# Queries and keys: rounded and subtracted over 128 rows, halves moved by transfers

## The chip, the core and the metric

One core of one Trainium2 chip. PE multiplies matrices, DVE and ACT work on tiles of 128 rows (partitions), POOL and SP here mostly issue transfers (DMAs). All are driven by instruction streams of their own, in an order fixed when the kernel is built, and wait for each other by semaphores. The metric is the device time of one execution in microseconds, the median of three runs.

## The reference

One step of a decoder layer in fp32, for 1024 prompt tokens and 8 x 8 sample tokens together (T = 1088 columns).

```python
xn = rmsnorm(x, norm1_g)
q, k, v, glu_a, glu_b, gate_a, gate_b = split(xn @ w_in)       # 16 query heads, 4 key heads of 64
attn = swa(q, k, v, sinks)                                      # window 128, a learned sink a head
c = dwconv31(glu_a * sigmoid(glu_b))                            # causal depthwise convolution
merged = sigmoid(gate_a) * (attn @ w_o_attn) + sigmoid(gate_b) * (silu(layernorm(c)) @ w_pb)
h = x + merged @ w_out
y = h + (silu(gate) * val) @ w_down                             # gate, val = dwconv3(rmsnorm(h) @ w_up)
return rmsnorm(y)                                               # and the new caches
```

## The kernel before

Every fp32 product is made of three matmuls in the rounded format fp32r: an operand is split in a high half (the value rounded) and a low half (the value minus the high half), and PE adds wh x xh, wh x xl and wl x xh (lines 201 to 203). A split is a cast on ACT and a subtract on DVE (`split_ps`, lines 230 and 231; for weights lines 182 and 183).

The first phase streams the columns of `w_in` as 128-wide weights through PE, each over the tokens in three chunks (0 to 384, 384 to 768, 768 to 1088), eight steps a chunk. The order of the weights is a table of letters: b and a (the two factors of the conv input), g (gates), q, k, v. It starts `b a q0 g q0`, five weights side by side while the input is being normed, and goes on `b a q0 q0 k0 b a v v g g ...`; later stand `q1 q1 q1 g q1 k1`. The digit is the head pair p (0 or 1), and a q weight holds two query heads j of it, one in rows 0 to 63 and one in rows 64 to 127. After the projections of a pair come its scores (lines 359 and 360: kd and kl times q), softmax (330 to 339), transposes (369, split at 231 into `pth` and `ptl`) and the product with v (381 to 388), between the weights that follow.

Scores take q with its high and low halves stacked over the 128 rows: in the tile `q0` (g = 0) the high half of the head is in rows 0 to 63 (`r` in the code) and the low half in rows 64 to 127 (`x`), in `q1` (g = 1) the other way round. `kd` holds the high half of a key head in both halves of the rows, `kl` the low half in both. So values have to change rows. Before, the engines do this by reading PSUM in one half of the rows and writing in the other (lines 730 and 731 for q, 751 to 755 for k). In the opening the scaled PSUM goes through a tile `qt` (line 834), which then stands for the PSUM.

Beside it run the conv of each channel group (chains on DVE at line 483; its input `u`, two buffers, is cleared by POOL at lines 662 and 663 and gets its history by the SP load `u<-cbT` at 664; its result goes out by POOL at 506 and 507) and the folds of the out weights (line 616, POOL copies and adds in memory). Weights are loaded by SP (`wraw<-wall`, line 159).

A scheduler sets the order in each engine's stream, from priorities and its own estimates; an instruction of a later weight can stand ahead of one of an earlier one. A tile has as many buffers as its pool says, and an instruction that writes a buffer waits for the last reader of it, a transfer included. SP and POOL issue their transfers in stream order, so one that waits holds up all behind it.

Of the kernel before, what the change touches and what calls it, by code (L numbers as in the profile page):

```python
# [6 lines left out]
F32 = mybir.dt.float32  # L7
F32R = mybir.dt.float32r
AF = mybir.ActivationFunctionType
ALU = mybir.AluOpType  # L10
AX = mybir.AxisListType

P = 128
# [107 lines left out]
class Build:  # L121
# [517 lines left out]
    def pool(self, es, name, side="right", bufs=1):  # L639
        return es.enter_context(self.tc.tile_pool(name=name, bufs=bufs, side=side, reuse_waits="tile"))  # L640

    def phase_x(self):
        nc, tc, a, pool = self.nc, self.tc, self.a, self.pool
# [5 lines left out]
        gl = pool(right, "gl")  # L649
# [56 lines left out]
        def gate_evac(kind, i):  # L706
# [8 lines left out]
                nc.gpsimd.dma_start(dst[i, :, o:o + n], t[:, :n])  # L715
            return ev

        def q_evac(p, j):
            st = states[p]
            if j == 0:  # L720
                st["q"] = [self.t(qp, [P, 4, T], f"q{g}", F32R) for g in range(2)]
                st["qs"] = self.t(qp, [P, NB // 2, 3 * 8 * NT], "qs")
                nc.gpsimd.memset(st["qs"], 0.0)

            def ev(c, o, n, ps):
                m = min(n, SEQ - o)
                for g in range(2):
                    r, x = [slice(y * HD, (y + 1) * HD) for y in (g, 1 - g)]
                    q = st["q"][g][:, j, o:o + m]
                    nc.scalar.copy(q[r], ps[r, :m])  # L730
                    nc.vector.tensor_tensor(q[x], ps[r, :m], q[r].bitcast(F32), ALU.subtract)  # L731
                if m < n:
                    for g in range(2):
                        r = slice(g * HD, (g + 1) * HD)
                        row = st["qs"].rearrange("p a (s x) -> p a s x", s=3)[r, :, 0:3:2]
                        nc.scalar.copy(row[:, :, :, (4 * g + j) * NT:(4 * g + j + 1) * NT],
                                       ps[r, m:n].rearrange("p (a s t) -> p a s t", a=NB // 2, s=2))
            return ev

        def do_k(p):  # L740
            st = states[p]
            st["ks"] = self.t(kv, [P, NS], "ks")
            st["kd"] = [self.t(kv, [P, SEQ], f"kd{g}", F32R) for g in range(2)]
            st["kl"] = [self.t(kv, [P, SEQ], f"kl{g}", F32R) for g in range(2)]

            def ev(c, o, n, ps):
                m = min(n, SEQ - o)
                for g in range(2):
                    r, x = [slice(y * HD, (y + 1) * HD) for y in (g, 1 - g)]
                    kd = st["kd"][g][:, o:o + m]  # L750
                    nc.scalar.copy(kd[r], ps[r, :m])
                    kl = st["kl"][g][:, o:o + m]
                    nc.vector.tensor_tensor(kl[r], ps[r, :m], kd[r].bitcast(F32), ALU.subtract)
                    nc.scalar.copy(kd[x], ps[r, :m])  # L754
                    nc.scalar.copy(kl[x], kl[r].bitcast(F32))
                if m < n:
                    nc.scalar.copy(st["ks"], ps[:, m:n])
                    kf = self.t(gl, [P, 384], "gt", bufs=2)[:, :WIN]
                    nc.scalar.copy(kf, ps[:, m - WIN:m])
                    nc.gpsimd.dma_start(a["o_kp"][p], kf)  # L760
                    nc.gpsimd.dma_start(a["o_kn"][p], st["ks"])

            self.stream(("k", p), xs, ev)
# [38 lines left out]
        p0_es = ExitStack()  # L802
        p0 = pool(p0_es, "p0", "left")
        put_q = [q_evac(0, j) for j in range(2)]
        spare = [q[:, 3, :DM] for q in states[0]["q"]]
        self.slot = lambda i: (None, spare) if i == 4 else (p0, "xy"[i - 2]) if 2 <= i < FIRST else (self.wp, i % 2)
# [32 lines left out]
        for c in range(3):  # L839
# [3 lines left out]
            r, steps = self.norm1_stats(p0, c, xr[c])  # L843
# [36 lines left out]
        for n, (kind, i) in enumerate(self.order[:self.n_in]):  # L880
# [16 lines left out]
            if kind == "b":  # L897
                u = do_b(i)
            elif kind == "a":
                do_a(i, u)  # L900
            elif kind in ("ga", "gb"):
                self.stream((kind, i), xs, gate_evac(kind, i))
            elif kind == "q":
                if i == (1, 0):
                    self.drain()
                self.stream((kind, i), xs, q_evac(*i))
            elif kind == "k":
                do_k(i)
                if i == 1:
                    plan_units(1)  # L910
            elif kind == "v":
                if i == 0:
                    do_v()
                    plan_units(0)
# [892 lines left out]
```

## Time and profile before

| | us |
|---|---|
| runs, median (lowest, highest) | 1663.01 (1662.69, 1663.13) |
| profiled execution | 1661.67 |
| its span | 1659.9 |
| PE busy | 1641.4 |
| DVE busy | 1338.7 |
| ACT busy | 892.3 |
| POOL busy | 318.4 |

A row of a group in the profile reads: line, engine, operation, output <- inputs, number; then durations in ns (smallest, median, largest) or the sum and the mean. A row of a timeline: start, duration, engine, line, operation, and in brackets the idle time ahead of it with what ended it. A row of a stretch gives the busy us of PE, weight loads, DVE, ACT and POOL with their numbers of instructions, then PE's granted clock, the DMA engines' share and GB/s. The granted clock is 1.00 in the stretches shown.

### The profile page before, as it was taken

The page shows a single profiled execution, that of the slowest core. Times are in us where ns is not written, and L with a number is a line of the kernel's source. Part 1 is how long each engine was busy: PE and PEld are TensorE (multiplying, and loading weights), DVE is VectorE, ACT ScalarE, POOL GpSimd, SP SyncE. Part 2 cuts the span into 40 slices and gives each one's busy share as a digit, 9 for nine tenths or more (in the row PEclk, how much of TensorE's full clock was granted, in tenths as well). Part 3 has the DMA queues.
Part 4 walks back from the last instruction along what each step waited for, and adds up shares of the span by engine and source line. Part 5 has one row for each costly group of instructions (what it writes and reads, how often), then busy time and mean ns, then how long its engine had stood idle before and what let it go on. Part 6 is the DMA issues. An engine that isn't in the chain of part 4 may idle for free.

```text
span 1659.9 us, 30349 instructions
## 1 busy us (share of the span) xinstructions
PE 1641.4 (99%) x11616; PEld 1623.9 (98%) x11616; DVE 1338.7 (81%) x2432; ACT 892.3 (54%) x1819; POOL 318.4 (19%) x589
## 2 busy tenths in 40 slices
PE   9999999999999999999999999999999999999998
PEld 9999899999999999999999999999999999999998
DVE  8999988999769995875676897877777778968546
ACT  7524377753388754993353564444444446834322
POOL 0400222151211211110000123333433221000050
PEclk9999999999999999999999999999999999999999
DMA  6122135163421255545346527676777544856473
GB/s 213 46 48 71 60 94 136 48 200 82 124 67 49 66 192 189 176 137 187 120 126 204 134 71 212 182 182 176 182 176 176 144 112 142 288 158 220 137 147 119
DMA packets 121746, 232.12 MB, mean 140 GB/s; under 512 B 25457, under 2 KB 68097, under 8 KB 121169
## 3 DMA queue, kind: packets, MB, share of 16 engines
q1 hardware_dynamic: 88496, 140.01, 27.4%
q0 software_dynamic: 32384, 89.51, 21.3%
q8 instruction: 91, 1.49, 0.4%
q10 hardware_dynamic: 720, 0.66, 0.1%
q14 instruction: 55, 0.44, 0.1%
HBM read 169.74 MB, written 89.62 MB: 156 GB/s over the span
## 4 chain that ended last, share of the span: by engine, by line
PE 83%; DVE 11%; ACT 3%; DMA 1%; issue 1%; SPq 0%; DVEq 0%; ACTq 0%
PE mm L201 20%; PE mm L202 20%; PE mm L203 20%; PE aux L201 6%; PE aux L203 6%; PE aux L202 6%; DVE c L483 3%; DVE bt L483 1%; PE aux L369 1%; DMA xr<-xT 1%; DVE q L731 1%; PE aux L359 1%; DVE wlo L183 1%; PE aux L381 1%; DVE xr L307 1%
## 5 line engine op out<-in xcount | busy, mean ns | idle before, releaser
L201 PE MATMUL mm<-xh,whi 128*128 128x384 f32 (+1 forms) x920 | 306.7, 333 | 2.9 <-ACT kd L754 1.6
L203 PE MATMUL mm<-xh,wlo 128*128 128x384 f32 (+1 forms) x920 | 300.6, 327 | 0.0
L202 PE MATMUL mm<-xl,whi 128*128 128x384 f32 (+1 forms) x920 | 300.5, 327 | 0.0
L201 PEld LDWEIGHTS mm<-xh,whi 128*128 128x128 f32 x920 | 173.0, 188 | 5.1 <-ACT kd L754 1.9
L202 PEld LDWEIGHTS mm<-xl,whi 128*128 128x128 f32 x920 | 173.2, 188 | 0.8
L203 PEld LDWEIGHTS mm<-xh,wlo 128*128 128x128 f32 x920 | 172.7, 188 | 0.1
L1225 DVE SCALAR_TENSOR_TENSOR acc<-st,fc,acc 128x1104 f32<-128x1104 f32 x88 | 119.5, 1362 | 8.7 <-ACT acc L1223 7.9
L182 ACT CAST whi<-wraw 128x1024 fp32r<-128x1024 f32 (+1 forms) x65 | 62.6, 969 | 55.8 <-PE mm L202 49.6
L483 DVE SCALAR_TENSOR_TENSOR bt<-u,consts,bt 128x513 f32<-128x513 f32 x120 | 89.7, 748 | 0.6
L483 DVE SCALAR_TENSOR_TENSOR c<-sm,hsum,c 128x512 f32<-128x512 f32 x120 | 89.5, 746 | 0.5
L183 DVE TENSOR_TENSOR wlo<-wraw,whi 128x1024 fp32r<-128x1024 f32 (+1 forms) x65 | 73.3, 1134 | 20.1 <-ACT whi L182 19.7
L483 DVE SCALAR_TENSOR_TENSOR c<-u,consts,c 128x512 f32<-128x512 f32 x112 | 83.5, 746 | 0.3
L230 ACT CAST wlo<-th 128x512 fp32r<-128x512 f32 x56 | 35.1, 626 | 65.1 <-PE aux L203 41.4
L1394 ACT COPY st<-mm 128x272 f32<-128x272 f32 (+2 forms) x133 | 44.4, 350 | 46.7 <-PE mm L203 46.7
L201 PE MATMUL mm<-th,whi 128*128 128x272 f32 x240 | 69.3, 289 | 0.0
L203 PE MATMUL mm<-th,whi 128*128 128x272 f32 x240 | 69.3, 289 | 0.0
L202 PE MATMUL mm<-tl,whi 128*128 128x272 f32 x240 | 69.1, 288 | 0.0
L335 ACT ACTIVATE p<-p,nm 128x257 f32<-128x257 f32 (+1 forms) x128 | 62.2, 490 | 12.0 <-DVE nm L330 11.2
L1373 DVE TENSOR_TENSOR st<-st,aux 128x272 f32<-128x272 f32 (+2 forms) x95 | 34.2, 379 | 38.0 <-PE aux L203 38.0
L203 PE MATMUL mm<-sh,wlo 128*128 128x384 f32 (+1 forms) x192 | 62.6, 326 | 0.0
L202 PE MATMUL mm<-sl,whi 128*128 128x384 f32 (+1 forms) x192 | 62.6, 326 | 0.0
L201 PE MATMUL mm<-sh,whi 128*128 128x384 f32 (+1 forms) x192 | 62.6, 326 | 0.0
(651 smaller groups left out, 5896.1 us busy)
## 6 DMA issues: line engine op xcount, KB each, us to landing
wraw<-wall SPq DMA_DIRECT2D x87, 512.0 KB, 3.9
d_x<-st POOLq DMA_DIRECT2D x27, 544.0 KB, 5.3
d_wd<-wall POOLq DMA_DIRECT2D x54, 256.0 KB, 6.2
th<-wall SPq DMA_DIRECT2D x18, 512.0 KB, 6.2
wraw<-wall SPq DMA_DIRECT2D x33, 256.0 KB, 4.3
x<-d_x SPq DMA_DIRECT2D x14, 544.0 KB, 4.6
d_x<-acc POOLq DMA_DIRECT2D x9, 816.0 KB, 7.3
d_wo<-wall POOLq DMA_DIRECT2D x24, 256.0 KB, 4.8
```

The lines of the kernel that those rows point to most:

```text
L182: self.nc.scalar.copy(h[:, z], r[:, z])
L183: self.nc.vector.tensor_tensor(l[:, z], r[:, z], h[:, z].bitcast(F32), ALU.subtract)
L201: mm(ps, wh, xh, start=first, stop=False, skip_group_check=more)
L202: mm(ps, wh, xl, start=False, stop=False, skip_group_check=more)
L203: mm(ps, wl, xh, start=False, stop=last, skip_group_check=more)
L230: self.nc.scalar.copy(h, src)
L307: nc.vector.scalar_tensor_tensor(x, x, self.c("g1", k), rstd[:, :CHUNKS[c][1]], ALU.mult, ALU.mult)
L335: nc.scalar.activation(pt[:, j, lo:width + 1], pt[:, j, lo:width + 1], AF.Exp, bias=nm[:, j:j + 1], scale=-1.0, accum_out=den[:, j:j + 1])
L483: mac = lambda o, x, w: nc.vector.scalar_tensor_tensor(o, x, w, o, ALU.mult, ALU.add)
L1225: self.last_tap = nc.vector.scalar_tensor_tensor(acc, st[:, k:k + AW], fw(f, k), acc, ALU.mult, ALU.add)
L1373: plus = lambda d, s: nc.vector.tensor_tensor(d, d, s, ALU.add)
L1394: op(d, r(ps))
```

## The change

A new function `both_parts` splits a chunk's PSUM (or `qt`) over all 128 rows into two tiles `qkh` and `qkl`, one buffer each: one cast and one subtract. Transfers issued by SP then carry 64-row halves of them to where they belong: four a chunk for q (high and low, for two g), eight a chunk for k (high and low, each to both halves of the rows, for two g). For a q chunk one cast on ACT and one subtract on DVE go, for a k chunk five casts or copies on ACT and one subtract on DVE. Over 24 q chunks and 6 k chunks these are 54 fewer on ACT and 30 fewer on DVE, and 144 transfers more. The copies of sample tokens (`qs`, `ks`) and the new caches stay on ACT.

The diff touches only this; the norm matmuls of the opening stand at the same places in both kernels.

```diff
+        def both_parts(ps, m):
+
+            h, l = [self.t(gl, [P, 384], f"qk{z}", F32R) for z in "hl"]
+            self.split_ps(h[:, :m], l[:, :m], ps[:, :m])
+            return h, l
+
         def q_evac(p, j):
...
                 m = min(n, SEQ - o)
+                parts = both_parts(ps, m)
                 for g in range(2):
                     r, x = [slice(y * HD, (y + 1) * HD) for y in (g, 1 - g)]
                     q = st["q"][g][:, j, o:o + m]
-                    nc.scalar.copy(q[r], ps[r, :m])
-                    nc.vector.tensor_tensor(q[x], ps[r, :m], q[r].bitcast(F32), ALU.subtract)
+                    for z, part in zip((r, x), parts):
+                        nc.sync.dma_start(q[z].bitcast(F32), part[r, :m].bitcast(F32))
...
                 m = min(n, SEQ - o)
+                parts = both_parts(ps, m)
                 for g in range(2):
                     r, x = [slice(y * HD, (y + 1) * HD) for y in (g, 1 - g)]
-                    kd = st["kd"][g][:, o:o + m]
-                    nc.scalar.copy(kd[r], ps[r, :m])
-                    kl = st["kl"][g][:, o:o + m]
-                    nc.vector.tensor_tensor(kl[r], ps[r, :m], kd[r].bitcast(F32), ALU.subtract)
-                    nc.scalar.copy(kd[x], ps[r, :m])
-                    nc.scalar.copy(kl[x], kl[r].bitcast(F32))
+                    for to, part in zip((st["kd"], st["kl"]), parts):
+                        for z in (r, x):
+                            nc.sync.dma_start(to[g][z, o:o + m].bitcast(F32), part[r, :m].bitcast(F32))
```

Line 664 and the lines up to 717 keep their numbers; below, the lines of the kernel after are 5 or 6 higher. The order on PE is the same in both kernels. On the other engines the scheduler has moved work; three places follow.

On DVE, at the first two chunks of the third query head of p=0 (mm is PSUM; c, bt, sm and u belong to the conv chain). Before:

```order
L483 SCALAR_TENSOR_TENSOR c_883<-sm_884,hsum_86,c_883 128x512
L483 SCALAR_TENSOR_TENSOR bt_885<-u_165,consts_77,bt_885 128x513
L731 TENSOR_TENSOR q_26_122<-mm_1203,q_26_122 64x384
L483 SCALAR_TENSOR_TENSOR c_883<-u_165,consts_77,c_883 128x512
L731 TENSOR_TENSOR q_27_123<-mm_1203,q_27_123 64x384
L483 SCALAR_TENSOR_TENSOR c_883<-sm_884,hsum_86,c_883 128x512
L483 SCALAR_TENSOR_TENSOR bt_885<-u_165,consts_77,bt_885 128x513
L483 SCALAR_TENSOR_TENSOR c_883<-u_165,consts_77,c_883 128x512
L731 TENSOR_TENSOR q_26_122<-mm_1232,q_26_122 64x384
L483 SCALAR_TENSOR_TENSOR c_883<-sm_884,hsum_86,c_883 128x512
L731 TENSOR_TENSOR q_27_123<-mm_1232,q_27_123 64x384
L483 SCALAR_TENSOR_TENSOR bt_885<-u_165,consts_77,bt_885 128x513
```

After:

```order
L483 SCALAR_TENSOR_TENSOR bt_909<-u_165,consts_77,bt_909 128x513
L483 SCALAR_TENSOR_TENSOR c_907<-u_165,consts_77,c_907 128x512
L231 TENSOR_TENSOR qkl_1253<-mm_1227,qkh_1252 128x384
L483 SCALAR_TENSOR_TENSOR c_907<-sm_908,hsum_86,c_907 128x512
L483 SCALAR_TENSOR_TENSOR bt_909<-u_165,consts_77,bt_909 128x513
L483 SCALAR_TENSOR_TENSOR c_907<-u_165,consts_77,c_907 128x512
L483 SCALAR_TENSOR_TENSOR c_907<-sm_908,hsum_86,c_907 128x512
L483 SCALAR_TENSOR_TENSOR bt_909<-u_165,consts_77,bt_909 128x513
L231 TENSOR_TENSOR qkl_1286<-mm_1260,qkh_1285 128x384
L483 SCALAR_TENSOR_TENSOR c_907<-u_165,consts_77,c_907 128x512
L483 SCALAR_TENSOR_TENSOR c_907<-sm_908,hsum_86,c_907 128x512
L483 SCALAR_TENSOR_TENSOR bt_909<-u_165,consts_77,bt_909 128x513
```

The two subtracts of a chunk with a conv row between them have become one, and conv rows stand where the second one was: between the subtracts of the two chunks there are five of them now, three before between the last of one and the first of the next. Ahead of the first `ptl` on DVE there stand 111 rows of line 483 before and 119 after.

On SP, at the last query head of p=1 and its keys. Before (the weights around the load of the last u of this stretch):

```order
L159 DMA wraw_4457<-wall 128x1024
L159 DMA wraw_4553<-wall 128x1024
L159 DMA wraw_4645<-wall 128x1024
L159 DMA wraw_4747<-wall 128x1024
L664 DMA u_5538<-cbT 128x8x30
L159 DMA wraw_4862<-wall 128x1024
L159 DMA wraw_5067<-wall 128x1024
```

After:

```order
L738 DMA q_548_4321<-qkl_4639 64x256
L738 DMA q_549_4322<-qkl_4639 64x256
L159 DMA wraw_4741<-wall 128x1024
L159 DMA wraw_4855<-wall 128x1024
L664 DMA u_5658<-cbT 128x8x30
L738 DMA q_548_4321<-qkh_4772 64x384
L738 DMA q_549_4322<-qkh_4772 64x384
L738 DMA q_548_4321<-qkl_4773 64x384
L738 DMA q_549_4322<-qkl_4773 64x384
L738 DMA q_548_4321<-qkh_4805 64x384
L738 DMA q_549_4322<-qkh_4805 64x384
L738 DMA q_548_4321<-qkl_4806 64x384
```

The four transfers of each chunk of that head (`qkh_4772` and `qkl_4773` are its first chunk's) and the eight of each chunk of k1 behind them stand after the load of `u`, where before only weights stood.

On POOL, at the conv store and the folds ahead of that load's memset (lines 662 and 663). Before:

```order
L616 DMA d_wo_65<-wall 128x512 x2
L507 DMA d_c_59<-u_4019 128x64
L616 DMA d_wo_65<-d_wo_65 16x4096
L616 DMA d_wo_65<-wall 128x512 x2
L506 DMA d_c_59<-u_4019 128x1024
L616 DMA d_wo_65<-wall 128x512
L662 MEMSET u_5538 128x30
L663 MEMSET u_5538 128x2
L616 DMA d_wo_65<-d_wo_65 16x4096
```

After:

```order
L507 DMA d_c_59<-u_4079 128x64
L616 DMA d_wo_65<-d_wo_65 16x4096
L506 DMA d_c_59<-u_4079 128x1024
L616 DMA d_wo_65<-wall 128x512
L715 DMA d_gb_61<-gt_4736 128x320
L616 DMA d_wo_65<-wall 128x512 x2
L616 DMA d_wo_65<-d_wo_65 16x4096
L662 MEMSET u_5658 128x30
L663 MEMSET u_5658 128x2
```

The stores of the conv result (507 and 506) and a fold's copy (`d_wo<-d_wo`) stand earlier against the moves from the weights (`d_wo<-wall`, a copy or an add), a gate's store stands behind them, and a second `d_wo<-d_wo` is now ahead of the memset.

## The prediction

> **What bounds the kernel.** I began with the first part of the page, busy time by engine.
>
> ```profile
> span 1659.9 us, 30349 instructions
> PE 1641.4 (99%) x11616; PEld 1623.9 (98%) x11616; DVE 1338.7 (81%) x2432; ACT 892.3 (54%) x1819; POOL 318.4 (19%) x589
> ```
>
> PE is busy for 1641.4 of 1659.9 us, and its 11616 matmuls stay as they are. The change can win only where PE waits, and can lose wherever PE is made to wait. The second view lists what PE waited for (total, number of times, longest).
>
> ```profile
> PE aux L359 <- DVE ptl L231: 3.5, 2, 3.0
> PE aux L299 <- DVE rows L314: 1.7, 2, 1.4
> PE mm L201 <- ACT kd L754: 1.6, 1, 1.6
> PE mm L201 <- ACT qs L736: 1.3, 1, 1.3
> ```
>
> The last two are waits for the lines that the change rewrites, so it is tempting to book 2.9 us. The third view, busy time by stretch (PE, weight loads, DVE, ACT, POOL), says why not.
>
> ```profile
> 100.00:120.00 20.00, 20.00 (x124) 20.00 (x123) 19.65 (x32) 3.69 (x7) 1.46 (x2) 1.00 0.22 34
> 120.00:140.00 20.00, 18.68 (x111) 18.11 (x110) 19.47 (x29) 9.01 (x20) 1.25 (x4) 1.00 0.28 87
> 140.00:160.00 20.00, 18.44 (x114) 18.12 (x113) 19.15 (x28) 11.50 (x24) 1.09 (x2) 1.00 0.25 76
> 180.00:200.00 20.00, 19.96 (x139) 19.23 (x138) 19.86 (x43) 10.39 (x32) 3.78 (x7) 1.00 0.24 70
> 200.00:220.00 20.00, 16.01 (x96) 14.39 (x95) 19.54 (x44) 15.15 (x41) 5.81 (x8) 1.00 0.18 64
> 260.00:300.00 40.00, 40.00 (x261) 38.96 (x260) 39.13 (x87) 31.16 (x80) 11.25 (x22) 1.00 0.42 110
> 400.00:440.00 40.00, 40.00 (x243) 40.00 (x242) 39.15 (x60) 11.79 (x26) 3.76 (x7) 1.00 0.25 75
> 440.00:460.00 20.00, 20.00 (x130) 20.00 (x129) 9.82 (x22) 12.60 (x26) 4.65 (x9) 1.00 0.69 159
> ```
>
> From 100 to 220 DVE has no idle time left (19.2 to 19.9 of each 20 us), PE has. So in this stretch DVE sets the pace, and the last place at which PE waits long for it is the one that counts: what PE loses earlier it would otherwise lose there. From 260 on PE is full in every stretch shown, so what is won before 260 stays won, unless a new wait appears. The timeline shows that last place.
>
> ```profile
> 202.91 0.33 PE L203 MATMUL mm<-xh,wlo 128*128 128x384 f32 x1
> 206.24 0.39 PE L359 MATMUL aux<-kd,q 128*128 128x256 f32 x1 [3.00 <-DVE ptl L231]
> ...
> 204.83 0.75 DVE L483 SCALAR_TENSOR_TENSOR c<-u,consts,c 128x512 f32<-128x512 f32 x1
> 205.50 0.69 DVE L231 TENSOR_TENSOR ptl<-aux,pth 128x512 fp32r<-128x512 f32 x1
> ```
>
> The attention of the first pair p=0 has begun; PE needs a bank that DVE's `ptl` still reads, and DVE reaches `ptl` only after a run of conv rows (L483), one each 0.665 us (204.83 to 205.50).
>
> **The DVE term, a gain.** The tiles q, kd and kl give the prices.
>
> ```profile
> L730 ACT CAST q<-mm x36: 365/473/478, 101.4 to 446.7; 64x384 fp32r<-64x384 f32 x24, 64x256 fp32r<-64x256 f32 x12
> L731 DVE TENSOR_TENSOR q<-mm,q x36: 417/552/560, 109.5 to 447.1; 64x384 fp32r<-64x384 f32 x24, 64x256 fp32r<-64x256 f32 x12
> L753 DVE TENSOR_TENSOR kl<-mm,kd x12: 416/549/561, 135.1 to 459.4; 64x384 fp32r<-64x384 f32 x8, 64x256 fp32r<-64x256 f32 x4
> L754 ACT CAST kd<-mm x12: 353/472/480, 135.7 to 460.9; 64x384 fp32r<-64x384 f32 x8, 64x256 fp32r<-64x256 f32 x4
> ```
>
> A 64-row subtract becomes half of a 128-row one with as many elements to a row; the 128-row conv rows next to it are timed by their row length too, so I price the new one like one old one (0.55 us at 384, 0.42 at 256), and each chunk saves one subtract. Up to that `ptl` there are 15 chunks: three each of the two opening heads, of heads 2 and 3, and of k. Ten are 384 wide and five 256: 10 x 0.55 + 5 x 0.42 = 7.6 us. But the scheduler fills the place: ahead of this `ptl` stand 111 conv rows before and 119 after. Eight more of them take 8 x 0.665 = 5.3 us. What is left is 2.3 us, and I take 2.5, since several of the removed rows also came with a short wait for their own cast. At most the 3.0 us of the wait above can be won here, with 0.5 us more at its other entry (3.5 in total); at least nothing, if DVE now waits for transfers to free its tile. ACT loses 54 short casts; it is the bound nowhere in these stretches (3.7 to 15.2 of 20), so I cost them at nothing.
>
> **The transfers.** They are new: 144 on SP's queue, 4 to a q chunk and 8 to a k chunk. No transfer from tile to tile is in this trace, so their price comes from neighbours.
>
> ```profile
> 0.74 0.87 SPq L257 DMA_DIRECT2D xr<-xT  x2
> 1.66 0.42 SPq L255 DMA_DIRECT2D wraw<-wall  x1
> ```
>
> ```profile
> d_ga<-gt POOLq DMA_DIRECT2D x4, 192.0 KB, 2.6
> ...
> o_kp<-gt POOLq DMA_DIRECT2D x1, 64.0 KB, 1.8
> ```
>
> Issuing takes SP 0.43 us each, 0.45 with the step to the next. Landing took 1.8 us for 64 KB and 2.6 for 192 KB (medians of two stretches); a half of 64 x 384 has 98 KB and lies nearer the first: 1.8 us, at most 2.6. One page bears on both numbers: the Trainium skill, "DMA: Bandwidth & Descriptors", section "Anatomy of one DMA — SWDGE (gpsimd) path", gives a fixed 2.0 us plus bytes over 436 GB/s, 2.2 us for 98 KB as an estimate, inside the two rows; by that the chain below would be 1.6 us longer. The same table gives some 50 ns for a dispatch, on POOL's path, where SP's rows show 0.43 a transfer; by it the twelve issues in the chain below would take 4.8 us less, and the whole would come to 1662.
>
> On an idle queue the transfers are hidden: a chunk is 24 matmuls, about 4 us of PE (243 in 40 us from 400 to 440), and a chunk's high halves need cast 0.47, two issues 0.9 and landing 1.8 = 3.2 us before the next cast may overwrite `qkh`. There is one `qkh` and one `qkl`, however, so a chunk's transfers cannot be overtaken by the next chunk's cast, and they can land late.
>
> ```profile
> wraw<-wall SPq DMA_DIRECT2D x1, 512.0 KB, 7.2
> o_cbs<-u POOLq DMA_DIRECT2D x1, 120.0 KB, 6.2
> ```
>
> That is the stretch 100 to 120: beside the many small pieces of `o_cbs` a weight took 7.2 us. Heads 2 and 10 meet an `o_cbs` and may wait some us there; DVE then runs other rows or stands, and the lower bound of the gain (nothing) holds this.
>
> **The wait that is added: the second pair's first scores.** In SP's order after the change, the load of a conv history `u<-cbT` (L664 before) stands ahead of all transfers of the last q head of p=1 and of k1. That load waits for POOL's memset, and this for a chain of POOL's own transfers. Before, nothing that PE needed soon stood behind it. The rows are the timeline's, of DVE, POOL, SP, ACT and PE in turn, and last the page's on the add's landing.
>
> ```profile
> 438.17 0.25 DVE L502 TENSOR_SCALAR u<-c,consts 128x64 f32<-128x64 f32 x1
> ...
> 438.96 0.56 POOL L507 DMA_DIRECT2D d_c<-u  x1 [3.51 <-DVE u L502]
> 439.51 0.51 POOL L616 DMA_DIRECT2D d_wo<-d_wo  x1
> ...
> 443.26 0.82 POOL L616 DMA_DIRECT2D d_wo<-wall  x1 [0.92 <-DMA d_wo<-d_wo]
> 449.18 0.12 POOL L662 MEMSET u<- 128x30 f32 x1 [5.10 <-DMA d_c<-u]
> ...
> 450.58 0.52 POOL L616 DMA_DIRECT2D d_wo<-d_wo  x1 [1.24 <-DMA d_wo<-wall]
> ...
> 449.15 0.55 SPq L664 DMA_DIRECT2D u<-cbT  x1
> ...
> 448.29 0.47 ACT L751 CAST kd<-mm 64x384 fp32r<-64x384 f32 x1 [0.25 <-PE mm L203]
> ...
> 455.76 0.28 PE L359 MATMUL aux<-kd,q 128*128 128x256 f32 x1
> ...
> d_wo<-wall POOLq DMA_DIRECT2D x24, 256.0 KB, 4.8
> ```
>
> After the change the memset waits for L507's copy, then the fold, the add behind it, and the issue of the next fold. L502 at 438.2 comes some 2 us sooner, since DVE (39.15 of 40) has lost eight or nine subtracts of 0.55 us, less the stand at head 10: 436. L507 and the fold issued: 437.9. The fold lands 3.7 us later (439.51 to 443.26): 441.2 to 441.6. The add lands 4.8 us after its issue at the median, and 7.3 us in this stretch beside a 512 KB store (443.26 to 450.58): 446 to 449, and the store runs beside part of it now too. The next fold, memset and L664's own 0.55 make 1.2. So SP is free at t0 = 447 to 450; I take 448, nearer the median, since the store now starts before the fold has landed and is over sooner. (All in the clock of before; what is won at 206 moves both sides.)
>
> From t0 the single tiles make everything serial. High halves of the head's chunk 0: two issues and landing, 0.9 + 1.8 = 2.7; cast of chunk 1, 0.5; the same for chunk 1, to 5.9; cast 0.4; the same for chunk 2, to 9.0; cast of k's chunk 0, to 9.5. Meanwhile the low halves go out between them, the last at 8.2, landed at 10.0, so k's subtract ends at 10.6. SP issues four copies of k's high half, 9.5 to 11.3, then two of the low half, 12.2; landed at 14.0. The first scores L359 and L360 need those: ready at t0 + 14 = 462. PE was there at 455.76: a wait of 6 us. Its bounds: nothing where t0 is 442 or less; 10 us with t0 = 450 and landings of 2.3. At p=0 such a load also stands between two chunks of head 3, but there the scores are far off:
>
> ```profile
> L751 ACT CAST kd<-mm x12: 365/473/475, 134.3 to 458.8; 64x384 fp32r<-64x384 f32 x8, 64x256 fp32r<-64x256 f32 x4
> L359 PE MATMUL aux<-kd,q x128: 277/280/388, 185.6 to 587.2; 128*128 128x256 f32 x128
> ```
>
> The first cast of k0 stands at 134.3, the first scores at 185.6, and 51 us hold any such chain.
>
> Sum: -2.5 + 6 = +3.5 us, from a profiled execution of 1661.7 (span 1659.9), which is 1.3 below the median of the runs, 1663.0. So 1666.5.
>
> **Rivals.**
> - *Gain alone (faster).* Place: the load L664 and the first scores of p=1. If POOL's chain ends by t0 = 442, the wait is gone and the 2.5 to 3.5 us of the DVE term are left: 1660. It decides from t0 = 444: there the wait (2 us) no longer eats the gain. For it: DVE has lost up to nine subtracts, 4.6 us, by then, and I credit 2. Against it: two transfers in series at 3.7 and 4.8 or more.
> - *Nothing left.* The wait is about as long as the gain: t0 of 444 to 447, or t0 = 448 with SP's issues so short that the twelve in the chain lose 3 us. For it: the add at 4.8 and L502 a us earlier give 446. Against it: every issue on SP that is shown takes 0.42 or more. 1663.
> - *Longer waits.* Landings run at 2.6 and more, as the weight's 7.2 did, and heads 2, 10 and the k chunks hold PE's banks: 1.5 us for each of the two p=0 places where PE already waits (1.3 and 1.6), and 9 at the scores, no gain at `ptl`: +10, 1673.
> - The change not doing what it says: DVE's 30 rows fewer are certain from the order, so I give this no chance of its own.
>
> **Chances.** What this kernel's measurement tells from no change is about 0.2%, 3.3 us. My forecast, a net loss of 2 to 7 us: 0.42. Nothing left: 0.24. Gain alone: 0.22. Longer waits: 0.12. Slower by over 3.3 us comes from the upper two thirds of the forecast and from the longer waits: 0.42. Faster by over 3.3 us needs the gain alone at its upper end or something I have not seen: 0.20. Within: 0.38. The range 1658.5 to 1673 leaves out the top of the longer waits and gains beyond the rows of the wait list; the forecast's own range is 1665 to 1670.
>
> **What the profile after will show.** Right: PE's wait list has L359 waiting for a DMA into kd, kl or q, once, 4 to 9 us, at the second pair's first scores; the DVE count falls by 30; the wait for `ptl` near 205 shrinks from 3.0 to under 1; L664's issue at 446 to 449 less 2.5, with the q transfers right behind it. Wrong: no DMA in PE's wait list, or `ptl` still at 3 us (then the conv rows took everything), or long waits for qk tiles at heads 2 and 3.

## The result and the profile after

The changed kernel takes 1675.57 us (median of five runs, 1673.45 to 1675.81), the kernel before 1662.98 in the same runs: ratio 1.0074, 95% interval 1.0059 to 1.0089. It is slower by 12.6 us. The profiled execution has a span of 1671.7 us. The first part of its page:

```profile
span 1671.7 us, 30563 instructions
PE 1645.9 (98%) x11616; PEld 1627.8 (97%) x11616; DVE 1317.8 (79%) x2402; ACT 867.8 (52%) x1765; POOL 317.3 (19%) x589
```

DVE has 30 rows fewer and 20.9 us less to do, ACT 54 fewer and 24.5 us less. What PE waited for (total, times, longest):

```profile
PE aux L359 <- DMA kd<-qkh: 7.7, 1, 7.7
PE aux L359 <- DVE ptl L231: 3.0, 1, 3.0
PE aux L360 <- DMA kl<-qkl: 2.2, 1, 2.2
PE mm L201 <- DVE qkl L231: 1.2, 1, 1.2
```

The first and the third row are new: two waits for transfers into kd and kl. The PE timeline gives their place; the row at 203.08 is the place that the prediction called the last one that counts, at 206.24 before.

```profile
203.08 0.38 PE L359 MATMUL aux<-kd,q 128*128 128x256 f32 x1 [3.00 <-DVE ptl L231]
...
451.03 0.41 PE L201 MATMUL mm<-xh,whi 128*128 128x320 f32 x1 [1.20 <-DVE qkl L231]
...
462.56 0.58 PE L359 MATMUL aux<-kd,q 128*128 128x256 f32 x1 [7.74 <-DMA kd<-qkh]
465.37 0.55 PE L360 MATMUL aux<-kl,q 128*128 128x256 f32 x1 [2.23 <-DMA kl<-qkl]
```

PE's order is the same in both kernels, so each matmul can be compared with itself. After the change PE is 3.2 us ahead at 203 and 3.5 us ahead from some 260 to 415 us. Then it loses 15.4 us within 50 us, is 11.9 us behind, and stays there to the end (11.8). Of the 15.4, 10.0 are the two waits, some 3 are matmuls at half clock between and behind them, 1.5 lie around the wait for `qkl` at 451 and 0.9 in small delays before 440. Each profile is of one execution, and after their first 50 us the kernels below already differ from the kernel before by up to 1 us either way; a difference of that size in PE's lead says little. The stretches, in the columns of the prediction's:

```profile
120.00:140.00 20.00, 20.00 (x121) 20.00 (x120) 19.50 (x29) 6.53 (x11) 1.25 (x4) 1.00 0.68 181
140.00:160.00 20.00, 20.00 (x137) 20.00 (x136) 18.27 (x27) 6.46 (x13) 1.09 (x2) 1.00 0.49 137
200.00:220.00 20.00, 16.93 (x98) 16.14 (x98) 19.65 (x43) 14.38 (x37) 5.64 (x8) 0.91 0.18 64
400.00:440.00 40.00, 39.89 (x241) 38.86 (x239) 38.12 (x59) 8.79 (x20) 2.72 (x5) 1.00 0.48 124
440.00:460.00 20.00, 13.62 (x83) 13.04 (x81) 2.21 (x3) 2.68 (x6) 5.68 (x10) 0.92 0.90 220
460.00:480.00 20.00, 15.21 (x81) 14.95 (x82) 5.16 (x22) 9.85 (x32) 1.65 (x3) 0.74 0.60 162
```

From 120 to 160 PE's 2.9 us of idle time are gone. From 440 to 480 nothing computes much: DVE 7.4 of 40 us, ACT 12.5, PE 28.8. The DMA share is 0.90 in the first half. SP's own timeline shows what they wait for.

```profile
443.77 0.60 SPq L664 DMA_DIRECT2D u<-cbT  x1
444.46 1.26 SPq L738 DMA_DIRECT2D q<-qkh  x2
445.81 1.19 SPq L738 DMA_DIRECT2D q<-qkl  x2
450.40 1.10 SPq L738 DMA_DIRECT2D q<-qkh  x2
451.59 1.21 SPq L738 DMA_DIRECT2D q<-qkl  x2
455.90 1.10 SPq L738 DMA_DIRECT2D q<-qkh  x2
```

The load of `u` goes out at 443.77, and behind it the three chunks of the last head, 5.9 and 5.5 us apart. A 384 chunk takes PE about 4 us. At the first of these steps PE's end of the second chunk and the landing come at the same time (449.8); at the second, ACT's cast waits for the landing alone:

```profile
455.50 0.37 ACT L230 CAST qkh<-mm 128x256 fp32r<-128x256 f32 x1 [4.19 <-DMA q<-qkh]
```

The landings are long here (medians by group, 440 to 460):

```profile
q<-qkh SPq DMA_DIRECT2D x4, 96.0 KB, 4.7
q<-qkl SPq DMA_DIRECT2D x4, 96.0 KB, 4.7
...
d_wo<-wall POOLq DMA_DIRECT2D x6, 256.0 KB, 6.3
```

PE's granted clock (last column but two) after the wait:

```profile
440.00:449.00 9.00, 9.00 (x56) 9.00 (x55) 0.00 (x0) 0.00 (x0) 3.98 (x9) 1.00 1.04 281
462.00:465.00 3.00, 0.58 (x1) 0.28 (x1) 0.54 (x1) 1.59 (x3) 0.00 (x0) 0.50 0.45 111
465.00:470.00 5.00, 4.63 (x17) 4.67 (x18) 2.77 (x10) 2.36 (x7) 0.00 (x0) 0.50 0.63 156
470.00:472.00 2.00, 2.00 (x15) 2.00 (x14) 0.66 (x5) 1.05 (x6) 0.00 (x0) 0.89 0.66 150
```

After the wait PE runs at half clock until 470, so some 5 us of matmuls are done at half speed, 2.5 us more than at the full one.

### The profile page after: what moved, and what is told of

Read it like the earlier page. It is cut to its first block, busy times and chain, and to the rows that moved or that the text cites. A ratio compares the mean times of both kernels' runs of the same rounds, so it can differ in the third digit from the quotient of the medians.

```text
span 1671.7 us, 30563 instructions
## 1 busy us (share of the span) xinstructions
PE 1645.9 (98%) x11616; PEld 1627.8 (97%) x11616; DVE 1317.8 (79%) x2402; ACT 867.8 (52%) x1765; POOL 317.3 (19%) x589
## 4 chain that ended last, share of the span: by engine, by line
PE 86%; DVE 7%; DMA 4%; ACT 2%; issue 1%; SPq 1%; POOL 0%; DVEq 0%; ACTq 0%; POOLq 0%
PE mm L201 20%; PE mm L203 20%; PE mm L202 20%; PE aux L201 6%; PE aux L203 6%; PE aux L202 6%; DVE c L483 2%; PE aux L369 1%; DMA q<-qkl 1%; DVE bt L483 1%; DMA d_c<-u 1%; PE aux L359 1%; PE aux L381 1%; PE aux L360 1%; PE aux L382 1%
```

## Experiments

The theory after this reading (A in the texts below): the gain comes from p=0 and the loss from one chain at the first scores of p=1, in which single tiles make each chunk wait for the landing of the one before, started late by the load of `u`. Rivals: B, the mass of transfers fills the DMA engines; C, the load of `u` alone. Each kernel was timed beside the kernel before, whose median was 1662.98 beside the changed one, 1662.53 beside the next four of the table, 1662.88 beside the four after and 1662.68 beside the last two.

| kernel | median us | ratio, 95% interval | wait for kd, kl at the scores of p=1 |
|---|---|---|---|
| changed | 1675.57 | 1.0074 (1.0059 to 1.0089) | 7.7 + 2.2 |
| p=0 only | 1659.09 | 0.9979 (0.9970 to 0.9988) | 0 |
| p=1 only | 1677.80 | 1.0093 (1.0079 to 1.0107) | 10.0 + 2.2 |
| two buffers | 1660.64 | 0.9989 (0.9980 to 0.9997) | 3.1 |
| load of u on POOL | 1668.86 | 1.0043 (1.0030 to 1.0055) | 4.1 + 2.3 |
| folds moved | 1667.88 | 1.0028 (1.0017 to 1.0040) | 3.1 + 2.4 |
| PE kept busy | 1674.98 | 1.0074 (1.0061 to 1.0087) | filled, + 0.9 |
| p=0 only, two buffers | 1656.38 | 0.9964 (0.9951 to 0.9976) | 0 |
| k1 by engines, two buffers | 1656.75 | 0.9966 (0.9954 to 0.9979) | 0 |
| two buffers, folds moved | 1657.97 | 0.9974 (0.9964 to 0.9985) | 0 |
| q only, two buffers | 1657.27 | 0.9967 (0.9955 to 0.9980) | 0 |

**The two halves apart.** The evacuation chooses by head pair; the old lines stay for the other pair.

```diff
-                parts = both_parts(ps, m)
+                parts = both_parts(ps, m) if p in MOVED else None      # (0,) or (1,)
```

> The split over 128 rows with transfers for the first head pair (p=0) alone; p=1 by the engines as before. Theory A (the loss is one chain at the first scores of p=1; p=0 only gains): PE is 3.4 us ahead from 170 us on and stays so, 1659.6 (1658.5 to 1660.5), no DMA into kd, kl or q in PE's wait list. Rival B (the loss comes from the mass of transfers, wherever they are): about half of the loss is here too, 1666 or more.

> The transfers for the second head pair (p=1) alone; p=0 by the engines as before. Theory A: the whole loss without the gain, 1663.0 + 15.5 = 1678.5 (1676.5 to 1680.5), L359 waits 7 to 8 us for kd and L360 2 us for kl. Rival B: half of it, 1669 or less.

Measured: 1659.09, 3.4 us faster, and 1677.80, 15.3 us slower. Their sum, +11.8, is the whole change's 12.6 within the intervals. With p=0 alone PE's lead stays at 3.9 us from 260 to 500 us, so p=0's transfers cost nothing at p=1. With p=1 alone the wait for kd is 10.0 us, where I expected 7 to 8. B, as a matter of their number, falls.

**Two buffers.**

```diff
-            h, l = [self.t(gl, [P, 384], f"qk{z}", F32R) for z in "hl"]
+            h, l = [self.t(self.qk[0], [P, 384], f"qk{z}", F32R, bufs=self.qk[1]) for z in "hl"]   # kv, 2 after the opening
```

> qkh and qkl with two buffers each after the opening. Theory A (with single tiles each chunk's cast waits for the landing of the one before): the chain after the load of u loses about two of its four landings, at 4.7 us each beside the stores; the wait at the scores falls from 9.9 to about 5 us, 1667 (1665 to 1670). Rival B (the DMA engines are full there, share 1.09 from 442 to 449, and that sets the end of the chain): no more than 2 us better, 1673.5 to 1676.

Measured: 1660.64, 15 us less than the changed kernel and 6 less than I expected. The wait is down to one row, though the landings are longer than with single tiles (medians, 430 to 448):

```profile
PE aux L359 <- DMA kd<-qkh: 3.1, 1, 3.1
```

```profile
q<-qkh SPq DMA_DIRECT2D x4, 96.0 KB, 5.7
...
q<-qkh SPq DMA_DIRECT2D x2, 64.0 KB, 7.8
```

So a landing of 5 to 8 us does not by itself make the wait. Single tiles make it at two places. One is the chain behind the last load of `u`: from the load's end to the landed low half of k it takes 17.1 us with two buffers, 20.9 with single tiles. The other, which my expectation left out, is worth more: the load itself goes out at 435.52 and not at 443.77. PE's lead there (6.1 for 2.6 us) explains 3.5 us of that. Most of the other 4.7 come from the load of the `u` before this one, on SP at 393.41 in the changed kernel with a chunk's low halves behind it. DVE stands there for its tile (single tiles; two buffers), and so comes later to the conv result for whose store the last load waits:

```profile
399.69 0.56 DVE L231 TENSOR_TENSOR qkl<-mm,qkh 128x384 fp32r<-128x384 f32 x1 [8.87 <-DMA q<-qkl]
```

```profile
396.54 0.42 DVE L231 TENSOR_TENSOR qkl<-mm,qkh 128x256 fp32r<-128x256 f32 x1 [4.54 <-DMA q<-qkl]
```

The surprise has a second part at p=0, where PE is now 5.65 us ahead at the first scores and not 3.2 (0.7 of the difference is from the first 50 us). DVE's rows ahead of the first `ptl` tell why (before; after; two buffers), with their idle time last:

```profile
L731 DVE TENSOR_TENSOR q<-qt,q 64x384 fp32r<-64x384 f32 (+1 forms) x12 | 7.3, 611 | 0.3
L731 DVE TENSOR_TENSOR q<-mm,q 64x384 fp32r<-64x384 f32 (+1 forms) x12 | 6.1, 511 | 0.4
L753 DVE TENSOR_TENSOR kl<-mm,kd 64x384 fp32r<-64x384 f32 (+1 forms) x6 | 3.1, 511 | 0.8 <-ACT kd L751 0.7
```

```profile
L231 DVE TENSOR_TENSOR qkl<-mm,qkh 128x384 fp32r<-128x384 f32 (+1 forms) x9 | 4.6, 511 | 2.4 <-ACT qkh L230 1.7 <-DMA q<-qkl 0.5 <-DMA kl<-qkl 0.2
L231 DVE TENSOR_TENSOR qkl<-qt,qkh 128x384 fp32r<-128x384 f32 (+1 forms) x6 | 3.9, 645 | 0.2 <-DMA q<-qkl 0.2
```

```profile
L231 DVE TENSOR_TENSOR qkl<-mm,qkh 128x384 fp32r<-128x384 f32 (+1 forms) x9 | 4.5, 505 | 0.0
```

16.5 us of subtracts became 8.5, but with single tiles DVE also stood 2.4 us there, 0.7 for its own tile and 1.7 for ACT's cast, which waited in its turn for a landing (`q<-qkh`, at 110.89). With two buffers it hardly stands at these subtracts (0.2 us in all), and `ptl` starts at 199.86, for 202.35 with single tiles and 205.50 before.

**The load of u on another queue.**

```diff
-            nc.sync.dma_start(u_views(u)[:, :, 0:HIST], a["cbT"][i])
+            nc.gpsimd.dma_start(u_views(u)[:, :, 0:HIST], a["cbT"][i])
```

> The load of u's history is issued by POOL, so that no q or k transfer stands behind it on SP; single tiles. Theory A: the first transfers of the last head go out at about 436 in place of 444.5 and the single tiles still chain; the wait falls from 9.9 to 3 to 5 us, 1666 (1663 to 1669). Rival C (the load alone makes the loss): no wait at all, 1660. Rival B: landings stay at 4 to 5 us because of the conv store and the folds, and the wait is still 7 us or more, 1671 or more.

Measured: 1668.86, a wait of 6.4 us, longer than the 3 to 5 expected. The landings stay at 4.6 us and more (medians, 430 to 460), as B said of this run. The head's first chunk now goes out at 437.32, not 444.46, and ACT's timeline shows the single tile holding the next two casts:

```profile
434.41 0.48 ACT L230 CAST qkh<-mm 128x384 fp32r<-128x384 f32 x1 [1.00 <-PE mm L203]
442.44 0.48 ACT L230 CAST qkh<-mm 128x384 fp32r<-128x384 f32 x1 [7.55 <-DMA q<-qkh]
...
447.93 0.37 ACT L230 CAST qkh<-mm 128x256 fp32r<-128x256 f32 x1 [4.06 <-DMA q<-qkh]
```

C falls: without the load ahead the chain is still there. It starts 7 us sooner and keeps PE waiting 3.5 us less. PE was only 2.0 us ahead here before the scores, for 2.6 in the changed kernel at 440: at 7 us it had waited 1.6 us for the first weight's cast. From 50 us on it gained about as much as with single tiles elsewhere (3.1 us by 260).

**The folds moved out of the stretch**, single tiles. The numbers 25 to 31 are the six weights named below and the `a` ahead of them.

```diff
-            if FOLD_FROM <= n:
+            if FOLD_FROM <= n and not 25 <= n <= 31:
```

> The changed kernel with single tiles, but the folds of the out weights are not issued during the weights q1, q1, q1, g, q1, k1; they come later. If the folds (with the conv store) made the landings long, q landings of the last head of p=1 fall from 4.7 to about 2 us, the load of u is issued about 2 us sooner, and the chain of 21 us becomes 17 or less: 1668 (1665 to 1670). If the transfers and weights alone make them long, they stay above 4 us and the time at 1673 or more.

Measured: 1667.88, as expected. The landings (440 to 460) fall to

```profile
q<-qkh SPq DMA_DIRECT2D x4, 96.0 KB, 2.4
q<-qkl SPq DMA_DIRECT2D x4, 96.0 KB, 2.1
...
q<-qkl SPq DMA_DIRECT2D x2, 64.0 KB, 4.5
```

and the load of `u` is issued 3.4 us sooner. So the folds made the landings long and held the conv store for which that load waits; the last row, the head's last chunk, landed beside a weight and stayed long. The wait falls from 9.9 to 5.5 us, near the 6 of the prediction, whose landings were priced without folds beside them. The folds cost something where they went: PE waits 1.9 us for `red` at line 524 (1.3 in the other kernel below that moves them), and in no other kernel here.

**Is the half clock a cost of its own?**

```diff
                 ps = self.bank("aux").rearrange("p (a b) -> p a b", a=2)
+                for _ in range(32 if (p, blk, g, jj) == (1, 0, 0, 0) else 0):
+                    nc.tensor.matmul(ps[:, 0, :P], self.mean, self.mean, start=True, stop=True)
```

> The changed kernel with 32 extra matmuls of a constant, whose result is overwritten, on PE just before the first scores of p=1; they fill about 7 us of the wait and take nothing from other engines. If the half clock after the wait (0.50 from 462 to 470) costs time of its own, the granted clock stays at 1.00 and the time falls by 2 to 2.5 us to 1673.3 (1672.5 to 1674). If not, 1675.6.

Measured: 1674.98, with the interval of the changed kernel. The clock is at 1.00 after the scores now, though a bank wait of 2.7 us for DVE's `qkl` has cost half clock ahead of them:

```profile
449.00:456.00 7.00, 4.55 (x21) 4.55 (x22) 2.12 (x3) 1.09 (x4) 0.00 (x0) 0.76 0.73 151
456.00:470.00 14.00, 13.10 (x105) 12.93 (x104) 2.25 (x3) 2.07 (x4) 0.00 (x0) 1.00 0.56 149
470.00:480.00 10.00, 10.00 (x66) 9.72 (x65) 3.76 (x24) 7.46 (x28) 1.84 (x4) 1.00 0.59 171
```

Matmul by matmul PE is 2.9 us ahead of the changed kernel at 472 us, but 1.0 of them stood at 440 already, before the extra matmuls, and 1.9 go again by 495 in a wait for the second pair's `ptl` on DVE. So what was won at the scores was lost again behind them, and my 2 to 2.5 us do not come off the time. The run is not clean, because of the earlier dip: how much the clock alone costs stays open, and the 0.6 us here are within the interval.

**Versions that keep the gain.** The first has p=0 alone with two buffers, the second all of q and k0, the third everything with the folds moved, the fourth q alone.

> Transfers for p=0 alone, with two buffers of qkh and qkl after the opening; p=1 by the engines. With single tiles DVE waited 2 to 3 us for landings at the third head; two buffers took that away and PE was 5.65 us ahead. All of that stays: 1657.1 (1656 to 1658.2). If the two buffers only helped at p=1, 1659.2 as with single tiles.

> Two buffers, all of q and the keys of p=0 by transfers, only k1 by the engines. In the run with two buffers the last head's first chunk had landed 6 us before PE reached the first scores, so the keys at the end of the chain make the wait: no wait for a DMA here and 1657.1 (1656 to 1658.2). If the q transfers are late too, L359 waits for q and 1659 or more.

> All transfers, two buffers, and no folds issued during q1 to k1. If landings beside the folds (4 to 8 us with two buffers) are all that is left of the wait of 3.1 us, it goes: no wait for kd or kl over 0.5 us at the first scores of p=1, and the whole change keeps the gain of 5.65: 1657.2 (1656 to 1658.5). If the eight issues of k1 on SP at 0.6 us each still come too late, 1 to 2 us of wait with a half clock stay: 1660.

> Two buffers, all q by transfers, all k by the engines. Three subtracts of k0 are back on DVE ahead of the first ptl (1.5 us), and two conv rows fewer stand there (117 for 119, 1.3 us less). If the time is set by how much work the order puts ahead of ptl, 1656.9, as with k0 by transfers (1656.75). If each saved subtract counts by itself, 1658.3.

Measured: 1656.38, 1656.75, 1657.97 and 1657.27. The four intervals overlap; all are faster than before by 0.26 to 0.36%. None waits for kd or kl. So the keys at the end of the chain made what was left of the wait with two buffers, and without the folds it goes even with them. The last run speaks for the order ahead of `ptl` and against counting each saved subtract of k0: at the first scores PE was 6.0 us ahead, not less than the 5.6 of the run with k0 by transfers, with two conv rows fewer ahead of `ptl` (117 for 119). These are single executions, so it is a hint; by time alone, 1657.27 lies between the two expectations and tells little.

## Why the prediction was wrong

*What bounds the kernel: right.* DVE set the pace to 206 us: with fewer and then with unhindered DVE rows `ptl` came at 202.35 and 199.86. A gain made there stayed to 415 us.

*The DVE term: right sign, 2.5 forecast, 3.5 measured by PE's lead.* Its bound was wrong. I took the 3.0 us wait for `ptl` as the most that could be won. That wait is 3.0 in every kernel here with p=0 by transfers, except the q-only one (2.3); the place moves as a whole, because PE's waits at 120 to 160 us vanish and PE arrives sooner too. With two buffers 5.65 us were won. What I showed as the mark of being right, `ptl` under 1 us, did not come; the mark of being wrong, `ptl` still at 3 us, did, but its reading (the conv rows took everything) was false. The DVE waits that I gave to the lower bound were there, 2.4 us at heads 2, 3 and k.

*The transfers' price: the step that failed.* I took 1.8 us for a landing and 0.45 for an issue. Beside the folds landing took 4.7 and issue 0.59; alone 2.0 to 2.4. The profile counts a landing from the start of its issue, so my 0.9 + 1.8 for two issues and a landing counted one issue twice; with nothing beside them they take 0.5 + 2.2, the same 2.7, so this part of the sum was off only by what ran beside it. I had quoted rows of 6 to 7 us beside POOL transfers, and left them to another place and to a rival with a chance of 0.12. The stretch from 440 on already showed a DMA share of 0.69 before, and four `d_wo<-wall` at 6.7 us from 436 to 470, the very place where I put the chain.

*The added wait: place and single tiles right, 6 forecast, 9.9 measured.* The load's end came at 444.4, which is 446.9 on the clock of before (PE 2.5 us ahead), for 448. That was luck, because it waited for something else than I said. SP's wait list shows

```profile
SPq L664 <- DMA d_c<-u: 4.6, 1, 4.6
```

which is the landing of the large conv store, and not the memset behind the folds. The memset runs after the load:

```profile
447.62 0.15 POOL L662 MEMSET u<- 128x30 f32 x1
```

In the rows of before that I showed, too, the load (449.15) stands ahead of the memset (449.18), both behind that store. Nor did L502 come 2 us sooner: at 435.54 it stood where it was on the clock of before, since DVE had stood 8.87 us behind the previous load of `u`. The two errors cancelled. The chain from the load's end to the low half of k took 20.9 us (444.4 to 465.2), 14 in my sum: some 4 of the difference go with the folds (17.2 us in the run without them), and most of the other 3 with the last q chunk's low halves, which landed beside a weight in 4.5 us there and for which k's subtract waits.

*Left out of the sum:* the bank wait of 1.2 us at 451, where `qkl` was late by the same chain, the half clock (some 3 us), and 0.9 us before 440, whose cause stays open; I put all three at nothing without a reason. The sum of +3.5 was 9.1 us short of the 12.6: 3.9 are the longer wait and some 5 these terms, less 1 for the larger gain. The last 1 us is no more than single executions differ by. The Trainium skill, "TensorE: Matmul & The Clock Gate", section "Part 1: The HAM clock gate", says that an idle window of some 3.4 us takes PE to half clock and a busy one brings it back. The trace agrees on the first, 0.50 after the 7.7 us. The second took 5 us from 465.4. After the wait for `ptl` near 200 us, shorter than that window (3.0 us, 2.3 in the q-only run), it is not one answer: the clock fell for some us in ten of the twelve profiles (0.91 over 200 to 220 after) and stayed at 1.00 in two, among them the one of before; the measurement decides.

*The rivals.* "Longer waits" was the nearest, with its landings of 2.6 and more; it put 9 us at the scores, and took the gain at `ptl` away, which stayed. Its 1.5 us at each of two places at p=0 did not come. Its terms, twice 1.5 and 9, add up to 12 us, or 1675, and not to the 10 and 1673 that I wrote; the upper end of my range was that 1673.

## What to carry to other kernels

A staging tile that a transfer empties is held until the transfer has landed: with one buffer, the work behind goes at the pace of landings, so give it a second one before anything else. In a queue served in order, ask what stands behind a load that itself waits. Price a landing from rows of the stretch in which it will fall, with what the other queues move there, and not from a quiet one. Where one engine sets the pace, a wait of the engine that follows is no bound on the gain; count the work ahead of the place instead.

## What the runs showed of the hardware

A transfer between two tiles of 64 x 384 (96 KB) landed in 2.0 to 2.2 us with little beside it, in 4.7 beside folds and weights, and one of 64 KB in 7.8 where two buffers let more of them be in flight. SP took 0.6 us to issue one, where the loads of the opening took 0.43. A wait of PE of 2.3 to 3.0 us near 200 us left the clock at 1.00 in two of the twelve profiles and brought it down for some us in ten.
